# Six gate tiles of a hybrid encoder layer: from filler in the attention loops to three seven-product pairs ahead of them

## The chip, the cores and the metric

The kernel runs on one core of a Trainium2 chip. The metric is the device time of one execution in microseconds, over everything from the first to the last instruction and what lies around it. Instructions run on five engines with queues of their own: TensorE (PE in the profile, with its weight loads as PEld), VectorE (DVE), ScalarE (ACT), GpSimd (POOL) and SyncE (SP), which issues the DMAs.

## What is computed

One encoder layer over two sequences of 512 tokens (a prompt and a sample) with 1024 channels, all in float32:

```python
xn = rmsnorm(x);  mn = rmsnorm(mem)
u, q, k, v, xq, g = split(xn @ w_in)             # g: 3 x 1024 gate columns
y_s5   = z * sigmoid(z @ w_glu + b_glu)          # z = gelu(state space of u, both directions)
y_diff = rmsnorm((softmax(q1 k1) - lam * softmax(q2 k2)) @ v)   # 4 heads, RoPE on q, k
y_x    = softmax(xq @ mk) @ mv                   # 4 heads, memory of 256 tokens per sequence
merged = sum(sigmoid(g_n) * (y_n @ w_up[n]) for n in (s5, diff, x))
x = x + merged @ w_out
return rmsnorm(x + ffn(rmsnorm(x)))              # silu(gate) * up, then w_ffn_out
```

What the change concerns is `g = xn @ w_in[gate columns]`: 3072 columns, which the kernel takes as 24 gate tiles of 128 columns, each over all 1024 tokens.

## The kernel before, in words

**Products.** Float32 products are made from three matmuls each. `split` (L134, L135; with a scale L137, L138) writes the rounded high half of a tile on ACT and the remainder, the low half, on DVE. `weight` (L146) loads a tile of 128x1024 into `wf` and splits it into `wh` and `wl`. A product of a tile with x is then wh·xh + wh·xl + wl·xh for each of the eight slices k of the 1024 channels and each of the two sequences s: 8 x 2 x 3 = 48 matmuls of 128x512 for one tile of output columns. All matmuls appear under L66, transposes under L69. The normalized x stays in memory on the chip for the attention stages as the high and low halves `xh[k]`, `xl[k]` of 128x1024 (both sequences side by side).

**Order of the stages.** Norms and memory keys and values; the state space with its scan on DVE, with 18 of the 24 gate tiles placed by `gates(n)` between its parts so that PE has work; the GELU of its output (L504 to L513: load `zu` and `zy`, some six DVE and ACT operations per tile of 128x1024, then split into `zh`, `zl`, four tiles); the output gate, four tiles of 48/2 = 24 matmuls against `w_glu`, with a tanh each (L529), a product with z (L532) and a write to DRAM (`bD`, L533); the memory tiles (`memory`); cross attention; the standalone key projection `dk0` (`qk_units(0, False)`); differential attention; merges; the feed-forward network.

**Gate tiles.** `gates` and `gate_units` both run 48 matmuls, take tanh(0.5 g) on ACT into `gt` and write it to DRAM (`gD`); the merges load it again (`gl`). The last six tiles come from `gate_units`: two are in the filler queue of the cross attention, one stands by itself behind `dk0`, three are in the queue of the differential attention.

**The attention loops.** Here the order on PE is held as the program writes it (`PE.on`); elsewhere a scheduler orders the instructions. In the cross attention 32 steps (head, sequence, block of 128 queries) each issue a score two steps ahead, fill, transpose the finished softmax row, fill again, and every fourth step run the six products with the values (`oo`). `fill(n)` draws matmuls from generators in a queue (projections for later stages, in portions of 6 matmuls), so that PE does not wait for the softmax. One unit of `fill` is one matmul of 128x512. In the differential attention 32 steps issue a score (two maps), `fill(10)`, the transposes (`turn`), the products with the values (`outputs`), and `fill(10)`; at step 22 the loads of the state space's result for the first merge (`first_in`) are put into the queue behind the generator in work. The queue ends with `merges()`.

**Pieces of the feed-forward weights.** `prepare` and `half_piece` compute sums of `w_fo` blocks on POOL (L454), split them (L137, L138) and write them to DRAM for the seven-product scheme of the last stage; 16 pieces are done in the cross attention, 12 more later.

## Time and profile before

| | us |
|---|---|
| median of 3 runs | 1604.44 |
| lowest and highest run | 1603.48, 1605.61 |
| span of the profiled execution | 1603.0 |
| PE busy in it | 1587.1 |
| DVE, ACT, POOL busy in it | 1162.9, 640.0, 541.6 |
| output of the state space and output gate | about 318 to 370 |
| cross attention | about 375 to 495 |
| differential attention | about 518 to 730 |

The profiled execution's span runs from the first to the last instruction; its own time, of the same execution, isn't given beside it, and the median of the runs is 1.4 us above the span. A row of the timeline has the start, the duration, the engine, the line, the operation, output<-input with the program's names, the shape, and in brackets the idle time of the engine ahead of it with what ended it. Matmuls are pipelined, so the spacing of their starts counts and not the 0.39 us that each row shows.

### The profile page before, as it was taken

How to read it: one execution, taken by the hardware profiler on the slowest of the kernel's cores; microseconds unless marked ns; L12 is line 12 of the kernel's file. 1: busy time of each engine (PE TensorE's matmuls, PEld its weight loads, DVE VectorE, ACT ScalarE, POOL GpSimd, SP SyncE). 2: the span in 40 equal slices, each digit the busy share in tenths (PEclk: the TensorE clock that was granted, in tenths of full speed). 3: DMA queues.
4: the chain of work that ended last, by engine and by line, in shares of the span. 5: the costliest groups of instructions: out<-in, count | busy, mean ns of one | idle time of the engine just before them, and what ended most of it. 6: DMA issues, size and time to landing. Idle time of an engine off the chain costs nothing.

```text
span 1603.0 us, 21625 instructions
## 1 busy us (share of the span) xinstructions
PE 1587.1 (99%) x7838; PEld 1314.8 (82%) x7838; DVE 1162.9 (73%) x1856; ACT 640.0 (40%) x1142; POOL 541.6 (34%) x449
## 2 busy tenths in 40 slices
PE   9999999999999999999999999999999999999997
PEld 7888788888898778778878878888888888788877
DVE  7976996076773766776465678888898778988654
ACT  6544323274652455574133443332333323233323
POOL 0010100001333220300343367676665553444653
PEclk9999999999999999999999999999999999999998
DMA  9554523576762111244454432333323223986222
GB/s 366 173 160 150 179 95 125 180 273 201 252 224 102 54 47 40 73 156 140 145 190 132 144 118 80 131 119 129 121 106 118 79 88 119 344 332 198 80 66 106
DMA packets 104891, 237.86 MB, mean 148 GB/s; under 512 B 13520, under 2 KB 45008, under 8 KB 104784
## 3 DMA queue, kind: packets, MB, share of 16 engines
q1 hardware_dynamic: 104784, 236.47, 43.1%
q8 instruction: 62, 1.02, 0.3%
q14 instruction: 45, 0.37, 0.1%
HBM read 165.16 MB, written 71.27 MB: 147 GB/s over the span
## 4 chain that ended last, share of the span: by engine, by line
PE 87%; issue 4%; DVE 3%; DMA 3%; POOL 2%; ACT 0%; SPq 0%; POOLq 0%; DVEq 0%; ACTq 0%
PE bkmm L66 75%; PE bksc L66 3%; PE bktr L66 2%; PE bkoo L66 2%; PE bktr L69 2%; DVE tl L135 1%; PE bktr L1626 1%; POOL mg L793 1%; PE bktr L1597 1%; DMA yt<-bD 1%; PE bktr L1686 0%; PE bktr L1687 0%; PE bktr L1685 0%; PE bktr L1565 0%; DMA acc<-in_w_fo 0%
## 5 line engine op out<-in xcount | busy, mean ns | idle before, releaser
L66 PE MATMUL bkmm<-xh,wh 128*128 128x512 f32 x640 | 255.4, 399 | 0.0
L66 PE MATMUL bkmm<-xh,wl 128*128 128x512 f32 x640 | 250.9, 392 | 0.0
L66 PE MATMUL bkmm<-xl,wh 128*128 128x512 f32 x640 | 250.5, 391 | 0.0
L66 PE MATMUL bkmm<-tl,wh 128*128 128x512 f32 (+1 forms) x621 | 241.2, 388 | 1.4 <-DVE tl L135 1.4
L66 PE MATMUL bkmm<-th,wl 128*128 128x512 f32 (+1 forms) x621 | 241.0, 389 | 0.9 <-DVE wl L135 0.9
L66 PE MATMUL bkmm<-th,wh 128*128 128x512 f32 (+1 forms) x621 | 241.1, 389 | 0.0
L134 ACT CAST wh<-wf 128x1024 fp32r<-128x1024 f32 (+1 forms) x134 | 117.9, 880 | 224.1 <-PE bkmm L66 179.8
L135 DVE TENSOR_TENSOR wl<-wf,wh 128x1024 fp32r<-128x1024 f32 (+1 forms) x134 | 145.1, 1083 | 50.2 <-ACT wh L134 45.7
L66 PEld LDWEIGHTS bkmm<-xh,wh 128*128 128x128 f32 x640 | 120.3, 188 | 30.3 <-issue 7.9
L66 PE MATMUL bkmm<-th,w 128*128 128x512 f32 x432 | 141.5, 392 | 2.7 <-DVE up L1101 1.0
L66 PEld LDWEIGHTS bkmm<-xh,wl 128*128 128x128 f32 x640 | 120.2, 188 | 26.7 <-issue 1.3
L66 PEld LDWEIGHTS bkmm<-xl,wh 128*128 128x128 f32 x640 | 120.4, 188 | 22.4 <-issue 0.4
L66 PEld LDWEIGHTS bkmm<-tl,wh 128*128 128x128 f32 x621 | 116.6, 188 | 25.9 <-DVE tl L135 2.1
L66 PEld LDWEIGHTS bkmm<-th,wl 128*128 128x128 f32 x621 | 116.5, 188 | 25.7 <-DVE wl L135 1.7
L66 PEld LDWEIGHTS bkmm<-th,wh 128*128 128x128 f32 x621 | 116.6, 188 | 23.9
L1165 POOL TENSOR_TENSOR up<-up,acc 128x512 f32<-128x512 f32 x44 | 83.6, 1920 | 87.8 <-DVE up L1101 87.8
L454 POOL TENSOR_TENSOR raw<-raw 128x128 f32<-128x128 f32 x28 | 15.2, 545 | 284.4 <-DVE nb L545 206.5
L66 PEld LDWEIGHTS bkmm<-th,w 128*128 128x128 f32 x432 | 80.9, 188 | 23.8 <-DVE up L1101 3.4
L793 POOL TENSOR_TENSOR mg<-mg,gl 128x1024 f32<-128x1024 f32 x16 | 43.5, 2720 | 139.0 <-DVE gl L789 139.0
L548 ACT ACTIVATE e<-bksc,nb 128x512 f32<-128x512 f32 (+1 forms) x96 | 58.8, 615 | 73.5 <-DVE nb L543 51.9
L66 PE MATMUL bkmm<-tl,w 128*128 128x512 f32 x216 | 84.2, 390 | 0.0
L66 PE MATMUL bkmm<-yh,wh 128*128 128x512 f32 x192 | 75.9, 397 | 0.8 <-ACT wh L134 0.4
(641 smaller groups left out, 3527.8 us busy)
## 6 DMA issues: line engine op xcount, KB each, us to landing
wf<-in_w_in SPq DMA_DIRECT2D x40, 512.0 KB, 3.9
wD<-hl SPq DMA_DIRECT2D x28, 512.0 KB, 2.9
w<-wD SPq DMA_DIRECT2D x28, 512.0 KB, 5.0
gD<-gt SPq DMA_DIRECT2D x24, 512.0 KB, 2.8
gl<-gD SPq DMA_DIRECT2D x24, 512.0 KB, 3.4
wf<-in_w_fg SPq DMA_DIRECT2D x22, 512.0 KB, 3.7
wf<-in_w_fu SPq DMA_DIRECT2D x22, 512.0 KB, 3.6
aD<-ac SPq DMA_DIRECT2D x22, 512.0 KB, 3.1
```

The source lines that it names most:

```text
L66: return self.put(self.eng.matmul(*args, **kw))
L69: return self.put(self.eng.transpose(*args, **kw))
L134: h = S.copy(hi, src)
L135: l_ = V.tensor_tensor(out=lo, in0=src, in1=hi.bitcast(F32), op=ALU.subtract)
L454: PO.tensor_tensor(out=a22, in0=a21, in1=a22, op=ALU.add)
L548: last_x = S.activation(out=e, in_=sc, func=AF.Exp, bias=nb, scale=scale, accum_out=sm)
L793: PO.tensor_tensor(out=mg[m], in0=mg[m], in1=gt, op=ALU.add)
L1165: PO.tensor_tensor(out=up, in0=up, in1=accs[s], op=ALU.mult)
L1597: PE.matmul(kp[64 * hf : 64 * hf + 48, g * 144 : (g + 1) * 144], l_[:, 2 * hf + g, :], o_[:, 4 * g4 + 2 * hf + g, :], start=(l_ is lr48), ...
L1626: PE.matmul(ps[:, g * P : (g + 1) * P], w_[:, gg * P : (gg + 1) * P], u_[:, 8 * o + gg, :], start=True, stop=True)
```

## The change

The last six gate tiles leave the filler queues. They are computed in a new stage between the output gate and the memory tiles, as three pairs. For a pair of tiles, x is taken as 2x2 blocks (two sequences by two halves of the channels) and the weights as 2x2 blocks (two halves of the channels by two tiles); the product is made from seven block products with sums and differences of blocks instead of eight. A block product is 4 slices x 3 = 12 matmuls of 128x512.

What that adds:

- a copy of the normalized x in DRAM (`xD`), written by eight DMAs of 512 KB early in the kernel, ahead of `next(s5)`; eight loads of it back (`differences(k)`, k = 0 to 3, each with four subtractions of 128x512 on DVE), and the split of the resulting tiles (`kept_in`, two of 128x1024 each). k = 0, 1 stand ahead of the GELU, k = 2 behind the gates that run beside it, k = 3 behind the output gate;
- for each pair two weight loads, two splits, four sums of weights (two on DVE, two on POOL), two more splits; seven products into three PSUM banks, four of which accumulate onto a result that ACT has copied out before; three additions on DVE, four tanh on ACT.

What it moves: the first 8 of the 16 pieces of `w_fo` go into the new stage; the RoPE tables are loaded behind it; the query projection `qk_units(1, True)` takes the place of the standalone gate tile; the first fill of a cross-attention step is 4 instead of 5 (8 instead of 9 once); the fills of the differential attention are 7 instead of 10 up to step 21.

```diff
     with queued():
+        for i in range(4):
+            nc.sync.dma_start(xD[:, 2 * i : 2 * i + 2, :L], xt[2][:, 2 * i : 2 * i + 2])
+            nc.sync.dma_start(xD[:, 2 * i : 2 * i + 2, L:], xt[3][i])
         next(s5)
...
-    rope = []
-    for nm in ("c", "s"):
...
+    def differences(k):
+        xa_, xb_ = slot("ld", name="xa"), slot("ld", name="xb")
+        nc.sync.dma_start(xa_, xD[:, k])
+        nc.sync.dma_start(xb_, xD[:, k + 4])
+        V.tensor_tensor(out=xa_[:, lo_], in0=xa_[:, hi_], in1=xa_[:, lo_], op=ALU.subtract)
+        V.tensor_tensor(out=xa_[:, hi_], in0=xb_[:, hi_], in1=xa_[:, hi_], op=ALU.subtract)
+        V.tensor_tensor(out=xb_[:, hi_], in0=xb_[:, hi_], in1=xa_[:, lo_], op=ALU.subtract)
+        V.tensor_tensor(out=xb_[:, lo_], in0=xb_[:, lo_], in1=xb_[:, hi_], op=ALU.subtract)
+        return [x_.rearrange("p (a n) -> p a n", a=2) for x_ in (xa_, xb_)]
+
+    def kept_in(tag, xa_, xb_):
+        th, tl = (slot(tag, [P, 4, L], F32R, n_) for n_ in ("tqh", "tql"))
+        split(th[:, 0:3:2], tl[:, 0:3:2], xa_)
+        split(th[:, 1:4:2], tl[:, 1:4:2], xb_[:, ::-1])
+        sums4.append((th, tl))
+
+    for k in range(2):
+        kept_in("tq", *differences(k))
     open_tags(phase, zt=2, zy=4, zs=8)
...
     gates(NG[2])
+    kept_in("tq", *differences(2))
...
         nc.sync.dma_start(bD[0, t], sg)
+    last_x = differences(3)
     phase.close()
...
+    prep = prepare(ges, pieces[: NPREP[0] // 2], "left")
...
+    def quad_gates(first):
+        ta, tb = next(todo), next(todo)
+        w = quad_weights(a["w_in"][20 + ta], a["w_in"][20 + tb])
...
+        pu, pv, pw = bank(), bank(), bank()
+        if first:
+            for ks in (range(3), range(3, 4)):
+                for p_, nm, o in ((pu, "A11", 0), (pv, "A12", 1), (pw, "S1", 3)):
+                    quad_product(p_, w[nm], o, ks)
+        else:
+            quad_product(pu, w["A11"], 0)
+            quad_product(pv, w["A12"], 1)
+        S.copy(ga[:, :L], pu)
+        plus(ga[:, :L], pv)
+        half_piece()
+        quad_product(pu, w["S2"], 4, more=True)
+        if not first:
+            quad_product(pw, w["S1"], 3)
+        gate(ga[:, :L])
+        S.copy(gb[:, L:], pw)
+        S.copy(ga[:, L:], pu)
+        half_piece()
+        quad_product(pu, w["S3"], 5, more=True)
+        half_piece()
+        quad_product(pw, w["S4"], 2, more=True)
+        plus(gb[:, L:], pu)
+        gate(gb[:, L:])
+        half_piece()
+        quad_product(pu, w["A22"], 6, more=True)
+        plus(ga[:, L:], pw)
+        gate(ga[:, L:])
+        gate(gb[:, :L], pu)
+        nc.sync.dma_start(gD[ta], ga)
+        nc.sync.dma_start(gD[tb], gb)
+        half_piece()
+
+    kept_in("tq", *last_x)
+    for i in range(3):
+        quad_gates(i == 0)
...
-    prep = prepare(pes, pieces[: NPREP[0]])
+    prep = prepare(pes, pieces[NPREP[0] // 2 : NPREP[0]])
...
-    queue += [xq[1], gate_units(), xq[2], xq[3], v_units(0, v0), gate_units(), units(a["w_in"][4], xh, xl, dq0.__setitem__)]
+    queue += [xq[1], xq[2], xq[3], v_units(0, v0), units(a["w_in"][4], xh, xl, dq0.__setitem__)]
...
-        fill(9 if i == 0 else 5)
+        fill(8 if i == 0 else 4)
...
-    for _ in gate_units():
+    for _ in qk_units(1, True):
         pass
...
-    queue += [qk_units(1, True), dk[1], gate_units(), qk_units(2, True), dk[2], v1_, qk_units(3, True), dk[3], gate_units(),
-              gate_units(), merges()]
+    queue += [dk[1], qk_units(2, True), dk[2], v1_, qk_units(3, True), dk[3], merges()]
...
-        fill(10 if i < n - 1 else 16)
+        fill(7 if i < 22 else 10 if i < n - 1 else 16)
...
-        fill(10)
+        fill(7 if i < 22 else 10)
```

More of the change, by code (lines that the diff above doesn't have):

```diff
@@ L495, in half_piece @@
             return next(prep, None)
+    qes = ExitStack()
+    open_tags(qes, side="right", tq=6)
+    sums4 = []
+    lo_, hi_ = slice(0, L), slice(L, NT)
+    def differences(k):
[14 more added lines that the diff above has]
+        kept_in("tq", *differences(k))
     open_tags(phase, zt=2, zy=4, zs=8)
@@ new lines, in quad_product @@
+    def quad_product(ps, w, o, ks=range(4), more=False):
+        nonlocal last_mm
+        mark = {"skip_group_check": True} if more else {}
+        for k in ks:
+            th, tl = quarter(k, o)
+            ws_ = slice(k * P, (k + 1) * P)
+            PE.matmul(ps, w[0][:, ws_], th, start=(k == 0 and not more), stop=False, **mark)
+            PE.matmul(ps, w[0][:, ws_], tl, start=False, stop=False, **mark)
+            last_mm = PE.matmul(ps, w[1][:, ws_], th, start=False, stop=(k == 3), **mark)
@@ L536, in encoder @@
+    kept_in("tq", *last_x)
+    for i in range(3):
+        quad_gates(i == 0)
+    while next(prep, 0) is None:
+        pass
+    ges.close()
+    qes.close()
+    res_ = ExitStack()
+    rpp = res_.enter_context(tc.tile_pool(name="rope", bufs=1, side="right", reuse_waits="tile"))
+    rope = []
+    for nm in ("c", "s"):
+        r_ = rpp.tile([P, L], F32, tag=f"r{nm}", name=f"r{nm}")
+        nc.sync.dma_start(r_, a["rope_" + nm])
+        rope.append(r_)
     last_x = None
```

50 lines of the change are left out of this document (36 added, 14 removed).

## The prediction

> **What bounds the kernel now.** I read the page first: busy shares, the granted clock, the chain of work that ended last, and then what TensorE (PE) waited for.
>
> ```profile
> span 1603.0 us, 21625 instructions
> PE 1587.1 (99%) x7838; PEld 1314.8 (82%) x7838; DVE 1162.9 (73%) x1856; ACT 640.0 (40%) x1142; POOL 541.6 (34%) x449
> PEclk9999999999999999999999999999999999999998
> DMA  9554523576762111244454432333323223986222
> PE 87%; issue 4%; DVE 3%; DMA 3%; POOL 2%; ACT 0%; SPq 0%; POOLq 0%; DVEq 0%; ACTq 0%
> PE bkmm L66 <- DVE tl L135: 1.4, 2, 0.8
> ```
>
> PE is busy 99% of the span, 87% of the last chain is PE, and the largest entry of its waits is 1.4 us. So PE is the bound almost everywhere: a matmul removed is worth its spacing, and the saving lasts only where the other engines still deliver in time. The stages that the change touches are full for PE; the windows tell how full the others are.
>
> ```profile
> 330.00:340.00 10.00, 10.00 (x46) 8.29 (x45) 9.79 (x17) 6.77 (x10) 0.00 (x0) 1.00 0.45 161
> 350.00:360.00 10.00, 10.00 (x48) 8.31 (x47) 5.24 (x12) 9.94 (x17) 0.00 (x0) 1.00 0.96 313
> 550.00:600.00 50.00, 50.00 (x267) 38.77 (x266) 35.34 (x69) 28.20 (x68) 11.92 (x8) 1.00 0.14 48
> 1592.00:1594.00 2.00, 1.32 (x12) 1.23 (x12) 1.90 (x5) 0.42 (x1) 2.00 (x4) 0.96 0.16 58
> 1594.00:1596.00 2.00, 1.36 (x6) 1.05 (x6) 0.22 (x2) 0.26 (x1) 0.69 (x2) 0.50 1.09 384
> ```
>
> After the span of a window come PE, weight loads, DVE, ACT, POOL, then clock, DMA share and GB/s. In 330 to 340 (the GELU of the state space's output) DVE has 9.79 of 10 us, in 350 to 360 ACT has 9.94 and the DMA share is 0.96: there three other engines stand at their limit beside PE. In the differential attention (550 to 600) DVE has 35.34 of 50.
>
> **The change, part by part.**
>
> *Matmuls.* The six gate tiles that ran as filler (two in the cross attention, one alone after it, three in the differential attention) were 6 x 48 = 288 matmuls of 128x512; three pairs with 7 x 12 are 252. The spacing, in a standalone gate (142 intervals between the first two rows) and in filler (22 between the last two):
>
> ```profile
> 315.44 0.40 PE L66 MATMUL bkmm<-xl,wh 128*128 128x512 f32 x1
> 347.64 0.39 PE L66 MATMUL bkmm<-xh,wl 128*128 128x512 f32 x1
> ...
> 489.06 0.40 PE L66 MATMUL bkmm<-xl,wh 128*128 128x512 f32 x1
> 494.09 0.39 PE L66 MATMUL bkmm<-xh,wl 128*128 128x512 f32 x1
> ```
>
> 32.20/142 = 0.2268 and 5.03/22 = 0.2286 us. Removed 288 x 0.2286 = 65.8, added 252 x 0.2268 = 57.2: **-8.6 us** (36 x 0.2268 = -8.2 at least). The seventh product's sums cost PE nothing: they are accumulated in PSUM or added by DVE.
>
> *Early copy of x.* Eight DMAs of 512 KB go out on SP's queue between the w_in loads and those of the state space's matrices. The line of DMA tenths has 9 in the first slice of 40 us and 5 in the second, where these 4.2 MB go out, so I take 2 us of delay for the matrices; all of it ahead of them would be, at the 366 GB/s of the first slice, 11.5 us. The scan is what waits for them, and it has room:
>
> ```profile
> 263.04 2.36 DVE L1678 COPY x<-st 64x2048 f32<-64x2048 f32 x2
> 271.99 0.38 PE L1685 MATMUL bktr<-u__1212,w__2711 128*128 128x128 f32 x2
> wf<-in_w_in SPq DMA_DIRECT2D x40, 512.0 KB, 3.9
> ```
>
> The last copy of the scan ends at 265.4, PE reaches its first use at 271.99: 6.6 us of cover. **0** (up to 11.5 - 6.6 = 4.9, if the cover is not enough). The rope tables are now loaded behind the new stage instead of ahead of the output gate; their first use is the row 493.16 below, over 80 us on: 0.
>
> *The stage before the new one (GELU and output gate).* DVE gets the differences of x and their low halves here. Rows for it:
>
> ```profile
> 324.33 1.29 DVE L506 SCALAR_TENSOR_TENSOR zy<-zu,vec,zy 128x1024 f32<-128x1024 f32 x1 [12.21 <-DMA zy<-yD]
> 329.69 1.22 DVE L135 TENSOR_TENSOR wl<-wf,wh 128x1024 fp32r<-128x1024 f32 x1
> 350.88 0.68 DVE L138 SCALAR_TENSOR_TENSOR zl<-zy,zh 128x512 fp32r<-128x512 f32 x1
> 493.16 0.69 DVE L752 TENSOR_TENSOR t<-bkmm,rc 128x512 f32<-128x512 f32 x1 [3.30 <-PE bkmm L66]
> 318.02 2.29 SPq L1692 DMA_DIRECT2D yD<-y__3002  x5
> 320.36 0.43 SPq L505 DMA_DIRECT2D zy<-yD  x1
> 347.86 0.39 PE L66 MATMUL bkmm<-zh,wh 128*128 128x512 f32 x1
> 366.37 0.69 ACT L529 ACTIVATE sg<-bkmm,bh 128x512 f32<-128x512 f32 x1 [5.75 <-DMA bD<-sg]
> ```
>
> The eight 512-wide differences of k = 0 and 1 fall into the 12.21 us in which DVE waits ahead of 324.33: free. Inside the chain stand four low halves of k = 0, 1 (4 x 1.22), four differences of k = 2 (4 x 0.69 at a spacing of 0.6) and its two low halves: 4.6 + 2.4 + 2.3 = 9.3 us. Against that, the small operations on lambda (16 of them, some 2.3 us) move behind the stage, and z's first load is issued ahead of the last state-space outputs instead of behind them (320.36 stands behind the five writes from 318.02), so that the chain starts 4 to 5 us earlier, unless DVE's differences hold it. Net 2 to 3 us later than 350.88, where PE starts the output gate at 347.86 with no slack. The order of the changed program answers by interleaving tiles 0 and 1 and putting the products with the fourth z tile last; the price is that both weight buffers stay taken, and the third tile's weights are cast by an ACT that also waits for a memory tile whose load waits for a buffer. I take **+1.5** (0.3, if the reordering covers it; 4, if that cast is held for most of the 5.75 us that ACT waited for a DMA ahead of 366.37).
>
> *The new stage.* A pair lasts 84 x 0.2268 = 19.1 us. DVE per pair: two low halves of weights and two of sums (1.22 + 0.69 + 2 x 1.22), two sums and three additions at 0.69, 7.8 us, and under 10 of 19.1 with the w_fo half pieces; ACT casts, copies and takes tanh of 14 times 512 columns, at the 0.69 of row 366.37 9.7 us. Only the first pair's weights can be late, since their loads stand on SP's queue behind the output gate's writes. **+0.4** (0 to 2).
>
> *Cross attention, inside.* The first fill of a step falls from 5 to 4 units (from 9 to 8 once). By the rows of the next fence a step is a score (0.35), transposes (0.13 to 0.25), ten units (2.29) and a quarter of six products (0.35), some 3.2 us; it loses 0.23. Half of the w_fo pieces have left DVE, which needs some 1.6 us of a step for the softmax and the split and 0.69 for a piece. **+0.2** (0 to 1.5).
>
> *Cross attention, end.* The queue now holds 288 units; at nine to a step it is empty after step 28, and nothing is left for 29 to 32. On PE the order is: last score, three pairs of transposes, the last head's six products, dk0. Nothing can be moved ahead, the order being held by hand. The chain, in before:
>
> ```profile
> 482.25 0.28 PE L66 MATMUL bksc<-mkvh,qh 128*128 128x256 f32 x1
> 482.60 0.40 PE L66 MATMUL bkmm<-xh,wh 128*128 128x512 f32 x1
> ...
> 488.61 0.38 PE L69 MATMUL bktr<-ident,e 128*128 128x128 f32 x2
> ...
> 494.32 0.39 PE L66 MATMUL bkoo<-xpTh,mkvh 128*128 128x512 f32 x1
> ```
>
> ```profile
> 482.80 0.42 DVE L543 TENSOR_REDUCE nb<-bksc 128x1 f32<-128x256 f32 x1 [1.12 <-PE bksc L66]
> 484.31 0.35 DVE L703 TENSOR_SCALAR e<-e,r 128x256 f32<-128x256 f32 x1
> 489.43 0.42 DVE L135 TENSOR_TENSOR xpTl<-bktr,xpTh 128x256 fp32r<-128x256 f32 x1
> ```
>
> From the score to the scaled row 484.66 - 482.25 = 2.41 us, in which PE has its score (0.35) and two ready pairs of transposes (0.25 to 0.3): idle 1.8. From the transpose to the low half 489.85 - 488.61 = 1.24, in which it has the pair itself and one product (0.13 + 0.23): idle 0.9. DVE and ACT also serve the two tiles before on the way, +0.4. **+3.1** (2.4 to 4). In before, 48 filler matmuls stand in these places (482.60 to 494.09), so this is a cost that the moved gates uncover.
>
> *The differential attention.* Fills go from 10 to 7 up to step 21:
>
> ```profile
> 560.73 0.50 PE L66 MATMUL bksc<-rh 64*128 64x512 f32 x2
> 564.47 0.60 PE L69 MATMUL bktr<-ident,e 128*128 128x128 f32 x4
> 568.22 0.50 PE L66 MATMUL bksc<-rh 64*128 64x512 f32 x2
> 575.77 0.50 PE L66 MATMUL bksc<-rh 64*128 64x512 f32 x2
> ```
>
> A step is about 7.3 us with 20 fills; six fewer (1.37) leave 5.94. DVE works 35.34/50 x 7.3 = 5.15 us of a step, less half a weight split: about 4.6 of 5.94. A score is transposed one step later; in before that leaves 3.5 to 6.2 us over the softmax, with seven instead of ten fills on either side 0 to 2.5. **+0.5** (0 to 2.5).
>
> *Entry of the merges.* The loads of the state space's tiles used to stand 14 gate units ahead of the first merge; now they stand directly before it, and low halves of the third branch's tiles stand on DVE's queue ahead of a softmax product, waiting for their own loads. **+0.6** (0 to 2.5).
>
> Sum: -8.6 + 1.5 + 0.4 + 0.2 + 3.1 + 0.5 + 0.6 = **-2.3 us**. On the span 1600.7; the median of the runs lies 1604.44 - 1603.0 = 1.4 above the profiled span, so **1602**. With every cost at its lower end, -8.6 + 2.7 = -5.9: 1598.5; with all six at their upper ends, 16.5: 1612 (and 1617 with the early copy's); these have separate causes, and I do not expect more than one or two at the top.
>
> [...] At the kernel's end the trace shows the granted clock fall from 0.96 to 0.50 within 2 us of thin PE work (1592 to 1596). [...]
>
> **The rivals.**
>
> *A: the saving stays.* ACT, DVE and the reordering cover all but the tail: -8.6 + 3.1 + 0.3 to 1.5 in the rest = -5.2 to -4: **1599.5**. For it: no wait over 1.4 us in before, DVE at 73%. Against it: 9.79 of 10 in one stage.
>
> *B (slower): the GELU chain starts no earlier.* If z's first load comes no sooner, or the differences wait for their copies and hold DVE's queue, the whole 9.3 - 2.3 = 7.0 us reach PE at the output gate instead of 1.5. -2.3 + 5.5 = +3.2, and up to +5: **1608 to 1609**. It decides from about 7 us of PE waiting between 345 and 372. For it: the DMA share of 0.94 to 0.96 around that stage, to which eight loads are added. Against it: the order on SP's queue.
>
> *C (slower): the differential attention becomes a softmax chain.* With no room left over the softmax, 22 steps lose 0.3 us each: 6.6 instead of 0.5, +3.8: **1608**. Against it: DVE at 4.6 of 5.94.
>
> *D: the clock.* The tail's hole halves the clock, as in 1594 to 1596, and it stays so about as long as the fall took there, 2 to 4 us: half of that is lost, +1 to +2: **1603 to 1604**. For it: the last products and transposes are as thin as the work before 1594. Against it: two holes with work between them. [...]
>
> *E: the change does not remove the work.* Excluded for the matmuls: the changed program has 252 in their place.
>
> **How the numbers follow.** Forecast (1600.5 to 1603.5) 0.45, A 0.28, D 0.07, B 0.10, C 0.10. 0.2% of 1604.4 is 3.2 us, about what a measurement of this kernel can tell from no change: faster means under 1601.2, slower over 1607.6. Faster: A and a third of the forecast, 0.28 + 0.14 = 0.42. Slower: most of B and C, 0.18. The rest, 0.40, is the same. The range, 1597 to 1608, reaches over A down to costs of about 1 us besides the tail's, and up to where B and C begin; it leaves out some 0.15 to 0.2. The likeliest case's own range is 1600.5 to 1603.5.
>
> **What the changed profile would show.** 36 fewer matmuls of 128x512, at the same spacing; a PE wait of 1 to 2 us on ACT's weight cast in the output gate; two holes in PE, 2 and 1 us, right before the standalone dk0, with DVE's row maximum and the low half as releasers, and the clock at 1.00 behind them; steps of 5.9 us in the differential attention with waits on the scaled row of a few tenths; under 1 us at the first merge. I am wrong if PE's waits together come to under 4 us (A), or if one stage alone takes more than 5 (B, C), or if the granted clock falls behind the cross attention (D).

## The result and the profile after

| | before | after |
|---|---|---|
| median of the runs, us (4 each, same chip) | 1604.18 (1603.48 to 1605.61) | 1631.81 (1628.73 to 1635.19) |
| ratio, 95% interval | | 1.0169 (1.0152 to 1.0186) |
| profiled span, us | 1603.0 | 1626.9 |
| first product of the output gate at | 347.86 | 349.31 |
| last product of the output gate at | 369.86 | 378.29 |
| first score of the cross attention at | 380.97 | 450.40 |
| first score of the differential attention at | 521.61 | 579.05 |
| first product of w_out at | 855.40 | 879.29 |

The changed kernel is slower by 27.6 us in the median, and by 23.9 us between the two profiled executions, which the following explains (the profiled execution of the changed kernel is the fastest of its four, 1628.73). The forecast was 1602. The page of the changed kernel: its span, the busy times, and the chain that ended last.

```profile
span 1626.9 us, 21679 instructions
PE 1587.9 (98%) x7802; PEld 1310.9 (81%) x7802; DVE 1209.3 (74%) x1901; ACT 656.9 (40%) x1165; POOL 553.7 (34%) x455
PE 72%; DVE 10%; issue 6%; DMA 5%; ACT 3%; POOL 3%; SPq 0%; POOLq 0%; ACTq 0%; DVEq 0%
```

PE has 36 matmuls fewer, as the change promises, and yet 0.8 us more of busy time (some matmuls start 0.43 us apart instead of 0.227, below) in a span that is 23.9 us longer. PE's share of the last chain falls from 87% to 72%, DVE's rises from 3% to 10%. The list of PE's waits (total, how often, longest), which began with 1.4 us in before:

```profile
PE bkmm L66 <- ACT wh L134: 5.3, 2, 3.4
PE bktr L69 <- DVE e L817: 3.5, 2, 2.1
PE bktr L69 <- DVE e L963: 3.4, 3, 2.6
PE bkmm L66 <- DVE nb L669: 3.1, 2, 1.9
PE bktr L69 <- DVE rs L199: 2.1, 3, 0.8
PE bkmm L66 <- DVE gl L903: 2.0, 1, 2.0
```

The first is in the output gate and the new stage, the second and fourth in the cross attention, the third and most of the fifth in the differential attention, the last in the merges.

**The account by stage.** What a stage lost is its length, less its length in before, corrected for the matmuls that came or went at the spacing of the prediction (252 x 0.2268 = 57.2 in the new stage; 96 x 0.2286 = 21.9 out of the cross attention and what stands up to the first differential score; 192 x 0.2286 = 43.9 out of the rest up to w_out). Output gate: 28.98 - 22.00 = 7.0. New stage: 72.11 - 11.11 - 57.15 = 3.9. Cross: 128.65 - 140.64 + 21.95 = 10.0. Differential attention and merges: 300.24 - 333.79 + 43.89 = 10.3. Start of the output gate: 1.45 later. Together 32.6, less the 8.7 of the matmuls: 23.9, the whole difference.

**Output gate.** PE and ACT in the timelines of the changed kernel:

```profile
359.96 0.39 PE L66 MATMUL bkmm<-zh,wl 128*128 128x512 f32 x1
363.73 0.80 PE L66 MATMUL bkmm<-zh,wh 128*128 128x512 f32 x1 [3.39 <-ACT wh L134]
...
366.51 0.63 PE L66 MATMUL bkmm<-zh,wh 128*128 128x512 f32 x1
366.94 0.63 PE L66 MATMUL bkmm<-zl,wh 128*128 128x512 f32 x1
...
370.55 0.40 PE L66 MATMUL bkmm<-zh,wh 128*128 128x512 f32 x1
```

```profile
360.87 1.06 ACT L239 ACTIVATE tk<-tk 128x1024 f32<-128x1024 f32 x1 [1.66 <-DMA tk<-in_memN]
...
361.93 1.25 ACT L549 ACTIVATE sg<-bkmm,bh 128x512 f32<-128x512 f32 x2
363.07 0.61 ACT L134 CAST wh<-wf 128x512 fp32r<-128x512 f32 x1
```

The third tile's weight cast (363.07) stands on ACT behind a memory tile's sum of squares (360.87), which waited 1.66 us for its load, and behind two tanh. PE has nothing for 3.39 us. Then its matmuls come every 0.43 us instead of 0.227 until 370.55: 15 rows and one missing record in 6.82 us, where 16 x 0.2268 = 3.6 would do, so 3.2 more. Hole and half clock make 6.6 of the stage's 7.0. The windows show the clock in this stage, the new stage and at the end of the cross attention, and how full the engines are in the two attentions (columns as in the prediction):

```profile
365.00:370.00 5.00, 4.89 (x12) 3.30 (x12) 4.23 (x10) 3.36 (x5) 0.00 (x0) 0.50 0.56 189
410.00:415.00 5.00, 4.45 (x12) 3.43 (x13) 2.87 (x5) 2.58 (x5) 3.05 (x4) 0.66 0.99 381
450.40:556.25 105.85, 98.74 (x593) 86.48 (x592) 73.51 (x222) 55.11 (x141) 20.31 (x34) 0.99 0.45 159
555.00:560.00 5.00, 5.00 (x17) 3.95 (x17) 2.04 (x4) 1.11 (x2) 0.00 (x0) 0.70 0.14 52
579.05:792.69 213.64, 206.78 (x1210) 163.35 (x1210) 166.83 (x311) 121.85 (x284) 33.73 (x24) 1.00 0.22 73
579.05:711.60 132.55, 130.09 (x803) 103.38 (x802) 108.02 (x205) 77.79 (x186) 30.02 (x22) 1.00 0.11 35
711.60:736.00 24.40, 20.01 (x108) 14.84 (x108) 24.18 (x41) 18.47 (x38) 3.70 (x2) 1.00 0.55 183
```

**Attentions.** The same stretches of before have PE busy all the time:

```profile
380.97:495.68 114.71, 114.71 (x672) 100.06 (x670) 82.57 (x218) 65.35 (x162) 33.59 (x65) 1.00 0.62 218
521.61:757.77 236.16, 236.16 (x1349) 189.59 (x1348) 165.15 (x312) 128.67 (x293) 36.54 (x24) 1.00 0.26 86
```

In the cross attention PE now stands still for 105.85 - 98.74 = 7.1 us, although DVE is busy for only 73.51 of 105.85, or 69%, less than the 72% of before; in the differential attention for 6.9 us, with DVE at 78% (70% in before). A busy share averaged over a loop does not tell this; the order on the queue does, or the share of a short stretch. A hole in the midst of the cross attention, PE first, then DVE:

```profile
500.19 0.39 PE L66 MATMUL bkmm<-wh,xh 128*128 128x256 f32 x1 [1.93 <-DVE nb L669]
```

```profile
497.98 1.22 DVE L135 TENSOR_TENSOR wl<-wf,wh 128x1024 fp32r<-128x1024 f32 x1
499.12 0.42 DVE L667 TENSOR_REDUCE nb<-bksc 128x1 f32<-128x256 f32 x1
499.46 0.68 DVE L135 TENSOR_TENSOR ql<-bkmm,qh 128x512 fp32r<-128x512 f32 x1
500.06 0.14 DVE L669 TENSOR_SCALAR nb<-nb 128x1 f32<-128x1 f32 x1
```

A low half of weights, 1.22 us, stands ahead of a row maximum and of a query's low half; PE goes on when these are done. In before, where each step has one unit of fill more, PE has no wait in this loop. The end of the cross attention, as forecast in kind:

```profile
553.00 0.41 PE L69 MATMUL bktr<-ident,e 128*128 128x128 f32 x2 [2.10 <-DVE e L817]
553.88 0.49 PE L66 MATMUL bkoo<-xpTh,mkvh 128*128 128x512 f32 x1 [0.46 <-ACT xpTh L134]
...
557.73 0.52 PE L66 MATMUL bkmm<-xh,wh 128*128 128x512 f32 x1
```

Holes of 2.10 and 0.46, and then nine intervals in 3.85 us, 0.428 each, where 2.04 us would do: 1.8 us of halved clock, the 0.70 in the window of 555. In the differential attention little is lost in the 132.55 us of steps with smaller fills (PE idle for 2.5), and 4.4 us in the 24.40 us at the entry of the merges, where DVE is busy for 24.18. The largest hole stands there, PE first, then DVE:

```profile
733.87 0.63 PE L69 MATMUL bktr<-ident,e 128*128 128x128 f32 x4 [2.60 <-DVE e L963]
```

```profile
729.34 1.20 DVE L138 SCALAR_TENSOR_TENSOR yl<-yt,yh 128x1024 fp32r<-128x1024 f32 x1
730.46 0.68 DVE L135 TENSOR_TENSOR wl<-wf,wh 128x512 fp32r<-128x512 f32 x1
...
731.19 1.27 DVE L667 TENSOR_REDUCE nb<-bksc 128x1 f32<-128x512 f32 x2
732.39 0.67 DVE L903 SCALAR_TENSOR_TENSOR mg<-gl,bkmm 128x512 f32<-128x512 f32 x1
732.99 0.74 DVE L963 SCALAR_TENSOR_TENSOR e<-e,r 128x512 f32<-128x512 f32 x1
```

The softmax product `e` (732.99), which the transposes at 733.87 need, stands on DVE behind the low half of a merge's tile (`yl`, of the third branch), a low half of weights (`wl`), the row maxima of the next score and a product of the merge (`mg`). ACT waits 3.61 us for a load ahead of 732.29, but the exponentials behind that wait belong to the next score, and the first of them ends at 733.93, when PE is already going on: this wait does not make the hole.

### The profile page after: what moved, and what is told of

The parts are those of the page before. It is cut to its first block, busy times and chain, and to the rows that moved or that the text cites. A ratio compares the mean times of both kernels' runs of the same rounds, so it can differ in the third digit from the quotient of the medians.

```text
span 1626.9 us, 21679 instructions
## 1 busy us (share of the span) xinstructions
PE 1587.9 (98%) x7802; PEld 1310.9 (81%) x7802; DVE 1209.3 (74%) x1901; ACT 656.9 (40%) x1165; POOL 553.7 (34%) x455
## 4 chain that ended last, share of the span: by engine, by line
PE 72%; DVE 10%; issue 6%; DMA 5%; ACT 3%; POOL 3%; SPq 0%; POOLq 0%; ACTq 0%; DVEq 0%
PE bkmm L66 63%; PE bktr L66 2%; DVE tl L135 1%; DMA wD<-hl 1%; PE bksc L66 1%; PE bkoo L66 1%; PE bktr L69 1%; DVE nb L667 1%; PE bktr L1739 1%; POOL mg L907 1%; DVE e L963 1%; ACT e L672 1%; DMA zu<-uD 1%; DVE wl L135 1%; DMA yt<-bD 1%
## 5 line engine op out<-in xcount | busy, mean ns | idle before, releaser
L66 PE MATMUL bkmm<-xh,wh 128*128 128x512 f32 x568 | 227.7, 401 | 2.0 <-ACT wh L134 2.0
L66 PE MATMUL bkmm<-xh,wl 128*128 128x512 f32 x568 | 222.3, 393 | 0.9 <-DVE wl L135 0.9
L66 PE MATMUL bkmm<-xl,wh 128*128 128x512 f32 x568 | 222.8, 392 | 0.0
L66 PEld LDWEIGHTS bkmm<-xh,wh 128*128 128x128 f32 x568 | 107.1, 188 | 29.0 <-issue 7.1
L66 PEld LDWEIGHTS bkmm<-xh,wl 128*128 128x128 f32 x568 | 106.8, 188 | 24.8 <-DVE wl L135 1.6
L66 PEld LDWEIGHTS bkmm<-xl,wh 128*128 128x128 f32 x568 | 107.2, 189 | 20.0 <-issue 0.4
L1277 ACT ACTIVATE ac<-gf 128x512 f32<-128x512 f32 x44 | 27.8, 633 | 181.1 <-DMA aD<-ac 93.8
L907 POOL TENSOR_TENSOR mg<-mg,gl 128x1024 f32<-128x1024 f32 x16 | 43.9, 2746 | 117.1 <-DVE gl L903 117.1
L869 POOL TENSOR_TENSOR t<-t,rs 128x512 f32<-128x512 f32 x16 | 23.7, 1482 | 175.2 <-DVE t L868 149.5
```

The source lines that it names most:

```text
L66: return self.put(self.eng.matmul(*args, **kw))
L869: PO.tensor_tensor(out=t2, in0=t2, in1=rope[1], op=ALU.mult)
L907: PO.tensor_tensor(out=mg[m], in0=mg[m], in1=gt, op=ALU.add)
L1277: last_t = S.activation(out=ac[:, cs], in_=gf, func=AF.Tanh, scale=0.5)
```

## The experiments

All were timed beside before (1603.9 to 1604.2). The first table has the times, the second what each stage lost in the profile, by the account above ("start" is how much later the output gate begins than in before; the matmul column is what the moved or removed matmuls make; the columns in between add up to the last, up to rounding).

| kernel | median (lowest, highest) | ratio to before, 95% |
|---|---|---|
| after | 1631.8 (1628.7, 1635.2) | 1.0152 to 1.0186 |
| e1, ordinary tiles | 1624.6 (1623.6, 1626.7) | 1.0112 to 1.0146 |
| e2, filler kept | 1676.3 (1674.7, 1677.0) | 1.0430 to 1.0462 |
| e3, memory tiles first | 1633.7 (1631.2, 1637.4) | 1.0164 to 1.0203 |
| e4, no pieces in the stage | 1637.2 (1632.5, 1641.1) | 1.0177 to 1.0228 |
| e5, half the differences | 1632.3 (1631.2, 1633.8) | 1.0161 to 1.0191 |
| e6, third branch later | 1628.7 (1628.6, 1629.0) | 1.0138 to 1.0168 |
| e7, warm tail | 1632.1 (1630.8, 1633.9) | 1.0159 to 1.0190 |
| e8, all pieces in the stage | 1672.0 (1670.3, 1673.9) | 1.0402 to 1.0436 |
| e9, one pair | 1621.0 (1620.0, 1621.6) | 1.0086 to 1.0123 |
| e10, cross filler alone | 1618.3 (1617.6, 1621.0) | 1.0074 to 1.0106 |
| e11, differential filler alone | 1617.2 (1613.5, 1618.1) | 1.0055 to 1.0092 |
| e12, e4 and e5 | 1638.9 (1635.6, 1642.4) | 1.0193 to 1.0237 |

| kernel | start | output gate | new stage | cross | diff. and merges | rest | matmuls | span to before |
|---|---|---|---|---|---|---|---|---|
| after | 1.5 | 7.0 | 3.9 | 10.0 | 10.3 | 0.0 | -8.7 | 23.9 |
| e1 | -0.1 | 0.6 | 0.0 | 8.0 | 12.7 | -1.8 | -0.5 | 18.9 |
| e2 | 1.6 | 8.2 | 3.8 | 1.5 | 0.0 | -0.6 | 57.2 | 71.7 |
| e3 | 1.3 | 6.3 | 5.3 | 10.9 | 10.4 | 1.3 | -8.7 | 26.8 |
| e4 | 1.4 | 8.7 | 1.7 | 14.3 | 11.9 | 0.4 | -8.7 | 29.7 |
| e5 | 1.7 | 0.7 | 5.6 | 15.1 | 12.4 | -0.3 | -8.7 | 26.4 |
| e6 | 1.3 | 7.6 | 4.1 | 10.0 | 9.2 | 0.6 | -8.7 | 24.2 |
| e7 | 1.5 | 9.6 | 3.3 | 10.6 | 11.2 | 1.7 | -8.7 | 29.1 |
| e8 | 0.8 | 9.1 | 39.9 | 11.9 | 14.6 | 1.6 | -8.7 | 69.1 |
| e9 | 1.2 | 6.4 | 5.3 | 0.0 | 6.4 | -1.5 | -2.9 | 15.0 |
| e10 | 0.5 | 0.0 | 0.0 | 11.3 | 1.9 | -0.6 | -0.2 | 12.8 |
| e11 | 0.0 | 0.3 | 0.0 | 0.0 | 13.7 | -1.1 | -0.4 | 12.5 |
| e12 | 1.8 | 0.4 | 16.5 | 13.2 | 11.5 | 0.8 | -8.7 | 35.5 |

Each row of the second table is one execution. The last part of the kernel ("rest"), which no edit touches, moves by -1.8 to 1.7 from row to row, and a half clock behind a hole, which comes and goes at the same place (below), makes 1.7: differences of this size between two rows show nothing by themselves.

**The theory and its rival.** Theory: the six tiles were the cover of the attention loops, and the loops starve without them, whatever way the tiles are computed elsewhere. Rival: the scheme itself (its loads, differences, sums and pieces) takes the time.

### e1: the same move without the scheme

```diff
-    for i in range(3):
-        quad_gates(i == 0)
+    for i in range(6):
+        gates(1)
+        for _ in range(2 + i % 2):
+            half_piece()
```

The copy of x and the differences are left out as well.

> The six gate tiles stay in the new stage, but as ordinary tiles of 48 matmuls: no copy of x, no differences, no sums of weights. Fills, queues, the eight weight pieces and the rope loads are as in the changed kernel. Starved-loops theory (what costs is that 240 matmuls of filler left the attention loops, whatever computes them now): cross attention, differential attention and merges keep their 20 us of 1604.2 against the kernel before (9.9 + 10.35 by the traces), the output gate and the new stage cost under 2, so about 1622 to 1626. Scheme theory (the scheme's own work on VectorE, ScalarE and the DMA queue does the harm, in its stage and as a backlog behind it): 1604 to 1609, since that work is gone.

Measured: 20.5 us slower than before with the same number of matmuls. Nothing is lost up to the first cross score (0.5 us), and 8.0 + 12.7 = 20.7 in the loops, against 20.3 in after. So the loops' loss does not come from the scheme. What the scheme adds is the other part: 1.45 + 6.98 + 3.85 = 12.3 us ahead of the cross attention in after, against 0.5 here, for a saving of 8.7.

### e2: the scheme with the filler kept

```diff
-    queue += [xq[1], xq[2], xq[3], v_units(0, v0), units(a["w_in"][4], xh, xl, dq0.__setitem__)]
+    queue += [xq[1], gate_units(), xq[2], xq[3], v_units(0, v0), gate_units(), units(a["w_in"][4], xh, xl, dq0.__setitem__)]
...
-        fill(7 if i < 22 else 10 if i < n - 1 else 16)
+        fill(10 if i < n - 1 else 16)
```

The three pairs are computed as well and written to a place that nothing reads.

> The other corner: the three seven-product pairs run in the new stage, with all their loads, differences and pieces, but write to a scratch buffer, and the six gate tiles run as well where the kernel before has them, with its queues and fills (work that is done twice, 252 matmuls more than before). Starved-loops theory: 57.2 us for the matmuls and only the 1.45 + 7.1 + 3.75 us that the traces show ahead of the cross attention, so 1604.2 + 69.5 = about 1674, and the attention loops as long as before. Scheme theory: a backlog of VectorE and DMAs reaches into the loops too, 1680 to 1694.

Measured: 72.2 us slower, 57.2 of it the added matmuls. The loops lose 1.5 and 0.0; the stages ahead of them lose 13.6, much as in after (12.3). With e1 this separates the two parts from both sides.

### e10 and e11: one loop's filler at a time

e10 moves the two tiles of the cross attention, e11 the other four (the one behind `dk0`, whose place `qk_units(1, True)` takes, and three of the differential attention), as ordinary tiles. All 16 pieces stand in the cross attention, as in before.

```diff
-    for i in range(3):
-        quad_gates(i == 0)
+    gates(2)                # e10; gates(4) in e11
...
+    queue += [xq[1], gate_units(), xq[2], xq[3], v_units(0, v0), gate_units(), units(a["w_in"][4], xh, xl, dq0.__setitem__)]    # e11
+        fill(9 if i == 0 else 5)    # e11
...
+        fill(10 if i < n - 1 else 16)    # e10
```

> No seven products at all. Only the cross attention's two gate tiles go to the place of the new stage, as ordinary tiles, with the changed kernel's fills of 8 and 4 there; the other four tiles, the fills of 10 and all 16 pieces are as before. Starved-loops theory: the cross attention keeps its 8 to 10 us, the rest is as before: 1612 to 1614. If a loop suffers only from what the earlier loop leaves behind, the sum isn't additive and this costs under 4.

> The other half: the differential attention's three tiles and the one by itself go to the new stage as ordinary tiles, with the query projection in the place of the latter and fills of 7 up to step 21; the cross attention keeps its two tiles, fills and 16 pieces. Starved-loops theory: 10 to 13 us from the differential attention and the merges, 1614 to 1617; together with the cross attention's run the two costs come to the 20.5 of the six ordinary tiles.

The copy of x and the differences are left out, as in e1.

Measured: e10 14.4 us, e11 13.3 us slower, nearly all of each loss in its own loop (11.3 and 13.7), little or none in the other's (1.9 and 0.0). The 1.9 of e10 is one wait for `gl` in the merges, which after has too (2.0); in e11 it is 0.4. e10 came out 4 us above what was expected of it. Its loop lost 3.3 more than in e1, and the difference between the two is half of the pieces, which load DVE in the cross attention (in before the low halves of all 16 take 19.8 us of it); e4 shows a like price (4.3). That is about half of why the two together (27.7) exceed e1 (20.5); most of the rest lies in the differential part (1.9, and 1.0 more than in e1). In e11 PE waits for the scaled row of the softmax:

```profile
PE bktr L69 <- DVE e L960: 6.1, 4, 2.6
```

### e9: one pair only

```diff
-    for i in range(3):
-        quad_gates(i == 0)
+    quad_gates(True)
...
-        fill(7 if i < 22 else 10 if i < n - 1 else 16)
+        fill(9 if i < 22 else 10 if i < n - 1 else 16)
```

The second fill is 8; the cross attention keeps its tiles and takes all 16 pieces, the differential one gives two tiles.

> Dose: only one pair goes through the seven products, in the new stage; four gate tiles stay filler (two in the cross attention, the one by itself, one ahead of the merges), with the cross attention's fills as in the kernel before, 9 and 8 in the differential attention, and all 16 pieces in the cross attention. Additive model: 12 matmuls less (-2.7), the early copy +1.5, the output gate +7 to 8, the new stage +1, the differential attention +2 to 4 for its two tiles, the cross attention 0: 1612 to 1616 against 1604.0. If the harm came from the size of the new stage (its DMAs), and not from the filler and the output gate, it is 1605 or less.

Measured 1621.0, above that range. Output gate and start lose 7.6 (8.4 with three pairs), the stage 5.3 without any pieces in it, where 1 was expected, the differential loop 6.4 for two of its three tiles. The cross attention, which has its cover, loses nothing. The scheme's costs ahead of the loops did not shrink with the number of pairs: 13.0 us for a pair that saves 2.9.

### e3 and e5: the hole in the output gate

e3 puts the third pair of loads and its differences behind the memory tiles' sums of squares. e5 leaves out loads, differences and splits of k = 2 and 3 and uses those of k = 0 and 1 in their place.

```diff
     gates(NG[2])
-    kept_in("tq", *differences(2))
...
+    kept_in("tq", *differences(2))    # e3: here; e5: nowhere
     bh = rp.tile([P, 4], F32, tag="bh", name="bh")
...
-    last_x = differences(3)           # e5
...
-    kept_in("tq", *last_x)            # e5
+    sums4 += sums4[:2]                # e5
```

> Only the third pair of loads of x, its differences and its split are moved behind the memory's sums of squares, so that the memory tiles don't wait for the two buffers that these loads hold. Buffer theory (the weight cast of the output gate's third tile stands on ScalarE behind a memory tile that waits for a buffer): the hole of 3.39 us and the half clock behind it, some 3.1 us, are gone, about 1625. Rival (the GELU chain on VectorE is what is late): the hole stays over 2 us and the time within 2 us of the changed kernel's 1631.8.

> Left out: the loads, differences and splits for k = 2 and 3 (the products take those of k = 0 and 1 in their place), so that nothing of the scheme is loaded, subtracted or cast while the output gate runs; all matmuls stay. In-order theory (ScalarE stands in its queue at a cast that waits for one of the late loads, and the weight cast of the output gate's third tile behind it): the output gate's hole of 3.4 us and the half clock behind it go, the output gate takes 22 to 23.5 us instead of 29.0, the time is 1624 to 1627. Rival (the hole comes from the GELU chain that starts its low halves late because of k = 0 and 1): a hole of over 2 us stays and the time is above 1628.

In e3 the hole stays, 4.0 us long. ACT no longer waits for a memory tile; it waits for the differences:

```profile
360.45 1.05 ACT L134 CAST tqh<-xa 128x1024 fp32r<-128x1024 f32 x1 [2.71 <-DVE xa L503]
...
363.97 0.62 ACT L134 CAST wh<-wf 128x512 fp32r<-128x512 f32 x1
```

The theory that the memory tile's buffer was the cause fell: in both kernels a late tile stands ahead of the weight cast and holds it. In e5, without the late tiles, the hole is 0.43 long and the output gate loses 0.7 instead of 7.0, so they are the cause; that they act through ACT's queue is read from the rows of after and e3. But the time is that of after: the new stage loses 1.7 more and the cross attention 5.1 more, with new waits of PE (the second is followed by a half clock, 1.7 us):

```profile
PE bkmm L66 <- ACT ga L625: 3.2, 1, 3.2
PE bkmm L66 <- DVE ql L135: 2.6, 1, 2.6
```

### e4, e8, e12: the pieces

e4 takes the eight pieces out of the new stage (all 16 in the cross attention), e8 puts all 16 into it, e12 is e4 with the edit of e5.

```diff
-    prep = prepare(ges, pieces[: NPREP[0] // 2], "left")
-    next(prep)
+    prep = iter(())                                       # e4, e12
+    prep = prepare(ges, pieces[: NPREP[0]], "left")       # e8
```

> None of the 16 pieces of the last weights is prepared in the new stage; all are in the cross attention, as before. Piece theory (in the new stage a cast of weights stands on ScalarE behind pieces that wait for their own writes): the hole of 1.96 us at the second or third pair and the half clock behind it go, the stage loses about 3.5 us; VectorE and ScalarE get them back in the cross attention, where they cost 2 to 6: 1629 to 1635 in all, with the hole moved. Rival (the hole is the load of the weights itself): the new stage stays as it is, and the time rises by the cross attention's 2 to 6 us.

> All 16 pieces of the last weights are prepared in the new stage, none in the cross attention. Load theory (the holes inside the cross attention come from VectorE and ScalarE being held by pieces): the stretch from its first score to the differential attention's first goes from 128.6 to 122 to 124 us (118.7 would be free of stalls), with the hole at its end left; the new stage gets longer by 3 to 10 us for its queue of writes. Starved-loop theory (a softmax is simply longer than the filler that is left between its score and its transposes): the stretch stays at 127 to 129.

> The kernel without the differences for k = 2 and 3 (left out, as in the earlier run, where the output gate got 6.3 us shorter and the time stayed), and with all 16 pieces in the cross attention. Queue theory (the new stage's pieces, with their reads and writes on SyncE's queue ahead of the memory tiles and small loads, set when the cross attention can start, so an earlier start is lost again): without them the gain of 6.3 us stays, the new stage takes 68 to 70 us instead of 73.8, and against the kernel with no pieces there (1637.2) this one is 6 us faster, 1631. Rival (given back for another reason, such as the banks): the new stage takes 72 or more, and the time is above 1634.

e4: the stage loses 1.7 instead of 3.9, and the cross attention 14.3 instead of 10.0. The hole of 1.96 is gone (another, of 1.40, stands later in the stage), so it comes with the pieces, and they cost about twice as much where they go instead.

e8: the stage loses 39.9 us, far more than expected, nearly all in one wait, in which the pieces finish and PE has nothing left:

```profile
PE bksc L66 <- ACT mkvh L134: 36.9, 1, 36.9
```

Yet the cross attention, free of pieces, still loses 11.9. Its first 7 us, from 487.88 to about 495, run at half clock behind that hole (the window shows 0.50), which is some 3.5 of it; the holes at the value projection (1.3 and 1.2) and at its end stay, and 11.9 - 3.5 = 8.4 is what e1 lost there.

```profile
490.00:495.00 5.00, 5.00 (x13) 3.84 (x13) 3.75 (x9) 1.80 (x5) 0.00 (x0) 0.50 0.83 268
```

So the pieces are not what starves the cross attention with the tiles gone, though more of them make it worse (14.3 with all 16).

e12: not better than e4 and e5, but worse than both. A new hole of 6.67 us stands in the stage:

```profile
385.44 0.80 PE L66 MATMUL bkmm<-tqh,sw 128*128 128x512 f32 x1 [6.67 <-ACT sw L134]
```

```profile
384.34 1.99 ACT L134 CAST sw<-ws 128x1024 fp32r<-128x1024 f32 x2 [3.13 <-DMA bD<-sg]
```

The cast of the sums of weights waits for a write of the output gate. The theory that e5's gain was lost to the pieces' DMAs is not borne out, though this hole and another of 3.97 keep the run from deciding it. Each edit lets the scheduler sort ACT's and SP's queues anew; why e5 gives its 6.3 us back stays open.

### e6 and e7: single holes in the loops

```diff
-            if m == 2:
+            if m == 5:                      # e6: load of the third branch's tiles
...
+            if i == len(steps) - 1:
+                warm(8)                     # e7: useless matmuls into a bank that nothing reads
...
+        if i == len(steps):
+            warm(4)
```

> Only the load and split of the third branch's tiles for the merges is asked for three merge tiles later (at tile 5 instead of 2), behind the last softmaxes. In-order theory (ScalarE waits 3.6 us at a cast for a load, with two exponentials behind it, and TensorE's transposes wait 2.6 us for them): the hole of 2.6 us near the last steps goes; 2 to 3 us less, 1629. Rival (VectorE is simply full there, 5.0 of 5 us for 15 us): the hole shrinks by under 1 us or turns up a few us later, the time stays within 1 us of 1631.8.

> Work is added and none removed: 8 useless matmuls of 128x512 stand on TensorE ahead of the last transposes of the cross attention and 4 ahead of its last six products, where it waited 2.1 and 0.46 us; nobody reads their result. Clock theory (the hole halves the clock, and the matmuls behind it start every 0.43 us instead of 0.23 for 3.7 us): the added 2.7 us fill the hole, the clock stays at 1.00 and the stretch up to the differential attention gets 1 to 2 us shorter although it has more work. Rival (the slow spacing there is not the clock, or the hole is too short to matter): the stretch gets 0 to 0.5 us longer.

e6: the hole of 2.6 us at 733.87 is gone, and another, of 2.0 in after, is longer:

```profile
PE bkmm L66 <- DVE gl L903: 3.2, 1, 3.2
```

It is followed by a half clock (1.7 us), which the hole of 2.03 was not. At the entry of the merges (712.50 to 737.00) PE stands still for 0.9 us instead of 4.4, and DVE is busy for 21.89 of 24.50. The edit takes ACT's wait and DVE's low halves away together, so it does not choose between the two theories. The rows of after do, and for the rival: DVE is never idle from 729.34 to 733.73, and the exponentials behind ACT's wait belong to a later step. The differential part loses 9.2 instead of 10.3. The median is 3.1 us lower, but the intervals of the two ratios overlap; the place is shown, the size isn't.

e7, the end of the cross attention:

```profile
557.29 0.41 PE L69 MATMUL bktr<-ident,e 128*128 128x128 f32 x2 [0.25 <-DVE e L823]
...
558.47 0.39 PE L66 MATMUL bkoo<-xpTh,mkvh 128*128 128x512 f32 x1
558.70 0.42 PE L66 MATMUL bkoo<-xpTl,mkvh 128*128 128x512 f32 x1
```

The spacing stays at 0.23. From the last cross score to the first differential one it takes 27.49 us (554.24 to 581.73) instead of 29.10 (549.95 to 579.05), with 12 more matmuls of 0.227: 1.6 + 2.7 = 4.3 us of hole and half clock gone, as measured in after (2.56 + 1.8). The total shows nothing of it: this profile lost 2.6 more in the output gate, which the edit does not touch, and 2.2 more in the rest of the cross attention, 1.7 of it by a half clock behind a hole of 1.83 (502.97) that the hole of 1.93 at the same place of after did not have.

## Why the prediction was wrong

**Removed matmuls, -8.6: right.** 7838 - 7802 = 36 at the same spacing, 8.7 by the account.

**Early copy of x, 0: wrong by little.** The output gate starts 1.45 us later, and 1.6 in e2; e1, without copy and differences, starts on time. What part of this is the copy's was not measured by itself.

**Output gate, +1.5 (0.3 to 4): the mechanism was right, the size 7.0.** It was put as "the third tile's weights are cast by an ACT that also waits for a memory tile whose load waits for a buffer", and that row stands in the trace. It was priced at a part of an old wait of 5.75; the hole was 3.39, near the upper end, and the halved clock doubled it. e5 shows the late tiles as the cause; e3 shows that a tile of the differences holds the cast as well as a memory tile does.

**New stage, +0.4: 3.9.** The prediction summed busy times (under 10 of 19.1 us) and saw only the first pair's weights. The hole ahead of 410.55 and the half clock behind it come with the pieces: e4 takes 2.2 us of the stage's loss away. ACT and PE in after; the cast of a pair's weights stands behind a piece that waits for a write:

```profile
409.05 0.52 ACT L137 ACTIVATE hl<-raw 128x384 fp32r<-128x384 f32 x1 [0.73 <-DMA wD<-hl]
409.47 1.03 ACT L134 CAST wh<-wf 128x1024 fp32r<-128x1024 f32 x1
```

```profile
410.55 0.50 PE L66 MATMUL bkmm<-xh,wh 128*128 128x512 f32 x1 [1.96 <-ACT wh L134]
...
411.12 0.60 PE L66 MATMUL bkmm<-xh,wh 128*128 128x512 f32 x1
...
414.80 0.40 PE L66 MATMUL bkmm<-tql,sw 128*128 128x512 f32 x1
```

From 411.12 nine intervals take 3.68 us where 2.04 would do: 1.6 more.

**Cross attention, +0.2 inside and +3.1 at its end: 5.6 and 4.4.** The end was forecast well as a hole (2.56), without the clock (1.8). The inside failed: "it loses 0.23" of PE work per step was compared with DVE's busy time per step. In the rows from 497.98 to 500.06 a low half of weights of 1.22 us stands on DVE's queue ahead of the row maximum of a score that PE had begun at 497.53, so the step's chain came late by what stood ahead of it, not by a mean.

**Differential attention, +0.5, and entry of the merges, +0.6: 10.3 together.** The entry of the merges is the step that failed most. PE stands still there for 4.4 us (711.60 to 736.00), where at most 2.5 was allowed, and for 2.0 more in the merges behind. The prediction had the mechanism, low halves of the third branch's tiles on DVE ahead of a softmax product, and summed too little on it: with no gate tiles in between, the first merge and the last softmaxes meet on DVE, which is busy for 24.18 of 24.40 us. (The wait of the low halves for their loads, which the prediction added, is not what holds DVE.) In e6, with the low halves moved away, 0.9 of the 4.4 is left. The 2.0 behind is another late load: ACT waits 2.52 us for a tile of the second branch (830.91), DVE 2.70 for ACT's half of it (831.99), with the products of the gates behind it. The steps with smaller fills cost 2.5 us of idle PE, the upper end of their term. These 8.9 us are 8.1 more than in before; the other 2.2 of the 10.3 lie in PE's busy time and were not traced. That the tiles that stood ahead of the merges are what is missing there is borne out by the kernels that keep them: e2 and e10, with all tiles of this loop, have no hole at this entry, and e9, with one ahead of the merges, has two, of 1.43 and 1.81.

Rival C was nearest in size, and by luck: its 22 steps of 0.3 each did not come, the loss lies behind them. "DVE at 4.6 of 5.94", which held it back, was right in size (166.83 of 213.64 is 78%, 4.6 of 5.94 is 77%), and as an average of the loop it hid the stretch at 99%. e11 reproduces the loss without any scheme (13.7, with 4.4 us of idle PE at the same entry).

**The clock, rival D: dismissed wrongly.** It got 0.07, because the hole comes in two parts with work between them; the clock fell behind 2.10 and 0.46 all the same, and its price, 1 to 2 us, was right there (1.8). In after, a hole of 3.39, one of 1.96, and one of 2.10 with 0.46 soon after each were followed by matmuls at 0.43: 3.2 + 1.6 + 1.8 = 6.6 us. But holes of 1.93 (500.19), 2.03 (835.69) and 2.60 (733.87) left the spacing as it was. The other kernels show that the same hole can go either way. The hole of 2.10 at the end of the cross attention stands in eight profiles; the clock is halved behind it in after, e1, e3, e5, e6 and e8, and stays in e4 and e10. The windows of after and of e10 (columns as above):

```profile
553.00:558.00 5.00, 4.53 (x12) 3.25 (x13) 0.55 (x2) 1.49 (x3) 0.00 (x0) 0.66 0.22 85
```

```profile
507.00:512.00 5.00, 4.23 (x17) 3.02 (x18) 2.50 (x6) 1.05 (x3) 2.00 (x2) 1.00 0.59 235
```

So the length of a hole alone does not decide here: in after 1.96 us was enough and 2.60 was not. What decides is not shown by any run here.

**Rival A (1599.5) and rival B (1608 to 1609).** A fell: PE's waits passed its 4 us several times over. B's 7 us were reached in what the output gate lost (7.0, half of it as waiting), but by ACT's queue and the clock, not by a late GELU chain (the start moved by 1.45).

The main cause is shown: e1 and e2 separate some 20 us in the loops from 12 to 14 us ahead of them. What stays open is how the waits redistribute when one of them is mended (e5, e6, e7). No run spreads the filler that is left in another way over the steps, or keeps some of it for the entry of the merges, so how much of the 20 us belongs to this order of the queue, and not to the tiles, is not shown. No version here comes below the kernel before.

## What to carry to other kernels

Matmuls that fill a loop with a softmax chain are the cover of that chain: removing them is worth their spacing only as far as the chain, taken step by step in the order in which the operations stand on each engine, still arrives in time, and this must be read from what stands ahead of each link, or from the busy share of the short stretch where two stages meet, not from the average of a loop. A saving of 8.7 us in PE work paid neither for the 20 us of cover nor for the 12 us of extra loads and casts on queues that another stage waited for. Price a hole of some two microseconds or more on TensorE at its length and the clock that may fall behind it: here half clock followed 25 of 47 holes of 1.75 to 3.21 us and all 12 longer ones, at 1.7 us in 23 of these 37 cases and 3.4 in three. And do not read a difference of 1.7 us between two executions as an effect of an edit.

## What the runs showed of the hardware that had not been expected

- The clock behind a hole: 0.43 us spacing for 6.8, 3.7 and 3.9 us after holes of 3.39, 1.96 and 2.10 + 0.46 (the granted clock of after, added up over windows of 1 us, stood at 0.50 for 6.8, 3.4 and 3.4 us); for about 7 us after the 36.9 us of e8. In the first case it was halved from the first matmul on, in the second from 0.6 us after the restart on (410.55, 410.89, 411.12, then 0.4 apart).
- The same over all fourteen profiles, by the granted clock in windows of 1 us behind each hole of 1 us or more (from 20 us on, where the clock was full ahead of it): of 28 holes below 1.75 us none was followed by half clock, of 47 from 1.75 to 3.21 us 25 were, of 12 longer ones all were. The half clock lasted 3.4 us in 23 of these 37 cases, a cost of 1.7 us, and 6.8 us in three (e4, e7, e8, behind 3.35 to 3.55 us); in the others it was already there when PE went on. A hole of the same place and length differs from profile to profile: the one of 2.60 to 2.63 us ahead of the last softmaxes was followed by half clock in e1, e4, e5, e8 and e11, and not in after, e3, e7 and e12.
- One late tile on ACT's queue held a cast that has no part in it: the weight cast of the output gate stood behind a memory tile that waited 1.66 us in after (360.87), and behind a cast of the differences that waited 2.71 us in e3 (360.45), and TensorE was idle for 3.39 and 4.00 us; in e5, without these tiles, for 0.43. In after the cast was not waiting for its own weights: their load was issued at 352.70 and landed 3.9 us later, 6.5 us ahead of the cast (363.07), and PE had begun its last product ahead of the hole at 359.96.
